# Moving GpSimd's elementwise work of a two-layer attention trunk to VectorE and ScalarE

## The chip, the cores and the metric

The kernel runs on one NeuronCore of a Trainium2 chip. The metric is device time in microseconds of one execution. The engines are named as in the profile: PE (TensorE matmul) and PEld (its weight loads), DVE (VectorE), ACT (ScalarE), POOL (GpSimd) and SP (SyncE, which here only issues DMAs). Every engine works through its own instructions in the order in which they were issued.

## The reference

Two layers over a sequence of 2048 rows of 1024 columns, in float32. Each layer normalises and modulates its rows, projects them, runs four heads of a gated linear recurrence (GLA) and four heads of differential softmax attention over all earlier rows, gates both with a SiLU, and projects the result back onto the rows.

```
for l in range(DEPTH):
    shift, scale, gate = split(silu(c) @ w_ada[l] + b_ada[l], 3)
    h = rms_norm(x, norm_g[l]) * (1 + scale) + shift
    gq, gk, gv, glr, gz, dq, dk, dv, dz = split_columns(h @ w_in[l])
    o_gla  = rms_norm(recurrence(gq, gk, gv, glr), gla_norm_g) * silu(gz)
    o_diff = rms_norm((softmax(q1 k1) - lam * softmax(q2 k2)) v) * (1 - lam_init) * silu(dz)
             # q and k of every head are rms-normed over 64 columns first
    x = x + gate * (concatenate([o_gla, o_diff]) @ w_out[l])
```

## The kernel before

**Units.** A unit is 512 rows (`u` = 0 to 3, four tiles `t` of 128 rows) of one layer `l`. For each unit the rows are normalised and transposed (`h`), projected in seven pieces of 512 columns (items 0 to 3: one attention head each; 4 and 5: the GLA's q, k and v; 6: its gate), put through the recurrence and the attention, and projected out in two halves of 512 columns (`out_gen`, items 7 and 8). Keys and values of earlier units come back from DRAM, so attention grows from unit 0 to unit 3.

**Split weights.** Dense products are made in three passes, `w` and `h` each being split into a rounded high part and the low part that is left: high by high, high by low, low by high. In unit 0 of a layer `weights` (L586) loads a piece `raw`, ACT rounds it into `hi`, POOL subtracts (`lo`, L596), and the pair is stored to DRAM (`wd`); units 1 to 3 load the finished pair. So `raw`, the 72 rounding casts of a layer and its 72 low parts stand in unit 0 alone.

**Roots.** GpSimd makes every reciprocal root with `pow(., -0.5)`: per tile of rows in `load_x` (xrs), per tile and head in `head_evac` (L910, `rq`, four columns), twice per unit in the recurrence (L868, `gw`, eight columns), and per query tile in the attention's `pv` (L1035, `wq`). In `head_evac` each tile's root is followed on DVE by the product that scales q and k (`rw`), and PE then transposes the four `rw`. In `gla_gen` the root `gw` is needed before the scaled output can leave PSUM into `osb` (the profile shows this buffer as `vN`).

**Gates.** `gate_proj` multiplies `osb` by the SiLU of the gate on POOL (L1107). `out_gen` multiplies each PSUM bank by the layer's `gate` on DVE into `t` and adds the residual `rt` on POOL (L1146 to L1152); in the last half of the last unit the add is on DVE. `gate` is itself made in four pieces by `ada_part(l, 2)`, which runs beside the projections.

**Order.** The code first only records instructions. Six generators (attention, q/k transposes, GLA, preparation, modulation, dense projections) are advanced against a rough clock (`run_streams`); `need` makes a generator wait until an event was recorded. `Program.order` then plays a list schedule with fixed costs and latencies per engine and issues everything in the order that comes out, so the order on every engine is fixed before the kernel runs, and a change of one instruction's engine re-plans the others. All DMAs are on SP's queue. `p_w` has four buffers of weight pairs, `p_raw` three, PSUM four accumulation banks (`acc`) and four for everything else (`sc`, `tp`, `po`).

In the profile nearly every instruction carries the line of the issuing helper (L305), so its tiles tell what it is: `w<-raw,w` is a low part, `rq<-qss,mhalf` a root, `rt<-t,rt` a residual add, `s<-s,r` the difference of the two softmax maps.

Of the kernel before, what the change touches and what calls it, by code (L numbers as in the profile page):

```python
# [11 lines left out]
F32 = mybir.dt.float32  # L12
F32R = mybir.dt.float32r
BF16 = mybir.dt.bfloat16
# [6 lines left out]
P = 128  # L21
# [287 lines left out]
def trunk_kernel(ctx, tc, x, c, w_ada, b_ada, norm_g, w_in, conv_w, w_gk, b_gk, gla_norm_g,  # L309
# [276 lines left out]
    def weights(l, u, item, k, src, n=None):  # L586
        w = p_w.tile([P, 2, 512], F32R, tag="w", name="w")
        hi, lo = w[:, 0, :], w[:, 1, :]
        kept = WD[l][item][k]
        if u > 0:  # L590
            SY.dma_start(w.bitcast(F32), kept)
            return hi, lo
        raw = p_raw.tile([P, 512], F32, tag="raw", name="raw")
        SY.dma_start(raw if n is None else raw.rearrange("p (g n) -> p g n", n=n), src)
        A.copy(hi, raw)
        G.tensor_tensor(lo, raw, hi.bitcast(F32), op=ALU.subtract)  # L596
        if NU > 1:
            SY.dma_start(kept, w.bitcast(F32))
        return hi, lo

    def silu2(dst, ps, shape=(P, 512)):
        th = t2(shape)
        A.activation(th, ps, AF.Tanh, scale=0.5)
        V.scalar_tensor_tensor(dst, th, 1.0, ps, op0=ALU.add, op1=ALU.mult)

# [124 lines left out]
    def gla_gen(l, u):  # L730
# [92 lines left out]
        for pr in range(TT // 2):  # L823
# [38 lines left out]
            for half in range(2):  # L862
# [13 lines left out]
        GL["osb"] = osb  # L876
        done("scan", key)
# [14 lines left out]
    def head_evac(l, u, hd, banks):  # L892
# [6 lines left out]
        for t in range(TT):  # L899
# [9 lines left out]
            V.tensor_scalar(ss[:, t, :], ss[:, t, :], 1.0 / 64, EPS, op0=ALU.mult, op1=ALU.add)  # L909
            G.tensor_tensor(rq[:, t, :], ss[:, t, :], mhalf[:, 0:4], op=ALU.pow)  # L910
            rv = rw.rearrange("p (a n) -> p a n", a=4)
            V.tensor_tensor(rv, rv, rq[:, t, :].unsqueeze(2).to_broadcast([P, 4, 64]), op=ALU.mult)
            qk.append(rw)
# [154 lines left out]
    def dense_gen(l, u, items):  # L1068
# [28 lines left out]
        def gate_proj():  # L1097
            banks = []
            yield from proj_N(lambda k: weights(l, u, 6, k, w_in[l, k * P:(k + 1) * P, C_GZ:C_GZ + 512]), banks)
            if LAST == 4:  # L1100
                done("free_h", key + 1)
            yield need("scan", key)
            osb = GL["osb"]
# [15 lines left out]
    def out_gen(l, u):  # L1119
# [3 lines left out]
        final = key == L * NU - 1  # L1123
        for hf in range(2):
# [119 lines left out]
```

## Time and profile before

| | |
|---|---|
| median of 3 runs | 2620.98 us (2617.81 to 2625.61) |
| the profiled execution, its own time | 2622.21 us |
| its span, first to last instruction | 2620.5 us |
| granted TensorE clock, mean | 0.992 |
| ACT busy | 1215.3 us (46%), 2592 instructions |
| HBM read, written | 362.29 MB, 111.15 MB |

The profile is of one execution; times of single instructions come from it. A group's row gives the number of instructions, the time in which at least one of them ran, the mean duration of one in ns, and, behind the second bar, how long the engine stood idle just before them and who ended that. Matmuls are pipelined, so their rows overlap. A row of stages gives, for each engine, busy time and number of instructions in a stretch of the span.

### The profile page before, as it was taken

What the parts mean: (1) busy time and instruction counts of PE and PEld (TensorE: products, weight loads), DVE (VectorE), ACT (ScalarE), POOL (GpSimd) and SP (SyncE); (2) the same over time, 40 slices, a digit from 0 to 9 for tenths busy, and PEclk for the clock granted to TensorE, in tenths of its full rate; (3) what the DMA queues carried; (4) which work ended last, traced back from release to release, by engine and by line L of the source; (5) the groups of instructions that cost most, each with busy time, mean ns of one, the idle gap of its engine ahead of it and who ended that gap; (6) DMA issues with size and microseconds to landing.
All of it is one profiled execution on the core that took longest, in us unless ns stands there. A gap on an engine that the chain in (4) does not pass through costs nothing.

```text
span 2620.5 us, 40701 instructions
## 1 busy us (share of the span) xinstructions
PE 2495.5 (95%) x13923; PEld 2031.5 (78%) x13923; DVE 1771.3 (68%) x5021; ACT 1215.3 (46%) x2592; POOL 608.3 (23%) x804
## 2 busy tenths in 40 slices
PE   6899899999999999999899999999999999999997
PEld 4676678877888778888677777888788887888786
DVE  4778847874667846677847874657737787377854
ACT  3555623554345543545634564344624556244442
POOL 2445421122010210102144554111111112110111
PEclk9999999999999999999999999999999999999998
DMA  8677586446553455344267767454374443743342
GB/s 283 225 235 256 200 302 198 161 166 211 178 181 125 158 171 189 133 140 149 81 237 248 245 214 253 169 179 156 126 268 155 143 157 113 254 141 129 101 149 89
DMA packets 201615, 476.11 MB, mean 182 GB/s; under 512 B 20736, under 2 KB 78272, under 8 KB 201408
## 3 DMA queue, kind: packets, MB, share of 16 engines
q1 hardware_dynamic: 201408, 473.51, 53.6%
q8 instruction: 111, 1.82, 0.3%
q14 instruction: 96, 0.79, 0.1%
HBM read 362.29 MB, written 111.15 MB: 181 GB/s over the span
## 4 chain that ended last, share of the span: by engine, by line
PE 71%; DVE 17%; DMA 3%; ACT 3%; issue 3%; POOL 1%; SPq 1%; DVEq 0%; ACTq 0%; POOLq 0%
PE acc L305 46%; PE sc L305 10%; PE po L305 8%; PE tp L305 7%; DVE s L305 6%; DVE t L305 3%; DMA wr<-in_w_ada_dram 1%; ACT s L305 1%; SPq L305 1%; DVE ql L305 1%; DVE am L305 1%; DVE hhi L305 1%; DMA w<-wd 1%; DVE r L305 1%; DVE hlo L305 1%
## 5 line engine op out<-in xcount | busy, mean ns | idle before, releaser
L305 PE MATMUL acc<-w,hhi 128*128 128x512 f32 x2560 | 835.0, 402 | 8.7 <-DMA w<-wd 4.3
L305 PEld LDWEIGHTS acc<-w,hhi 128*128 128x128 f32 x2560 | 464.8, 189 | 101.1 <-ACT ub L305 6.8
L305 PE MATMUL acc<-w,hlo 128*128 128x512 f32 x1280 | 504.9, 395 | 0.0
L305 ACT ACTIVATE s<-s,mx 128x512 f32<-128x512 f32 (+15 forms) x256 | 308.1, 1204 | 375.1 <-DVE s L305 372.3
L305 PE MATMUL acc<-hhi,w 128*128 128x512 f32 x1024 | 370.3, 402 | 0.6 <-DVE z L305 0.3
L305 PE MATMUL acc<-w,oh 128*128 128x512 f32 x1024 | 331.9, 401 | 12.1 <-DVE t L305 6.0
L305 DVE TENSOR_SCALAR_CACHE_REDUCE s<-sc,mx 64x64 f32<-64x64 f32 (+5 forms) x640 | 307.1, 485 | 37.8 <-PE sc L305 19.3
L305 POOL MEMSET s<- 64x64 f32 x256 | 38.9, 156 | 1111.1 <-DVE s L305 575.6
L305 PEld LDWEIGHTS acc<-w,hlo 128*128 128x128 f32 x1280 | 241.5, 189 | 48.9
L305 POOL TENSOR_TENSOR w<-raw,w 128x512 fp32r<-128x512 f32 x144 | 195.0, 1363 | 197.1 <-ACT w L305 180.7
L305 PEld LDWEIGHTS acc<-w,oh 128*128 128x128 f32 x1024 | 190.6, 190 | 55.8 <-DVE t L305 11.0
L305 PEld LDWEIGHTS acc<-hhi,w 128*128 128x128 f32 x1024 | 192.4, 188 | 37.7 <-DVE z L305 1.4
L305 PE MATMUL po<-Vj,aT 128*128 128x128 f32 x1536 | 207.9, 280 | 13.1 <-ACT aT L305 12.2
L305 PEld LDWEIGHTS po<-Vj,aT 128*128 128x128 f32 x1536 | 193.7, 195 | 24.6 <-ACT aT L305 18.9
L305 ACT COPY aT<-tp 128x512 f32<-128x512 f32 (+2 forms) x320 | 162.4, 520 | 94.1 <-PE tp L305 90.6
L305 PE MATMUL acc<-w,ol 128*128 128x512 f32 x512 | 202.8, 401 | 1.2 <-DVE ol L305 1.1
L305 DVE TENSOR_SCALAR_CACHE_REDUCE s<-sc 128x512 f32<-128x512 f32 (+4 forms) x256 | 158.6, 623 | 65.7 <-PE sc L305 61.6
L305 DVE SCALAR_TENSOR_TENSOR s<-s,r 128x512 f32<-128x512 f32 (+2 forms) x320 | 200.7, 677 | 3.1
L305 PE MATMUL acc<-hlo,w 128*128 128x512 f32 x512 | 200.9, 392 | 0.0
L305 PE MATMUL tp<-ident,s 128*128 128x128 f32 x1088 | 171.8, 275 | 16.9 <-DVE s L305 11.6
L305 POOL TENSOR_TENSOR rq<-qss,mhalf 128x4 f32<-128x4 f32 x128 | 129.8, 1032 | 215.4 <-DVE qss L305 215.3
L305 PEld LDWEIGHTS tp<-ident,s 128*128 128x128 f32 x1088 | 130.5, 140 | 55.4 <-issue 12.3
(177 smaller groups left out, 4064.7 us busy)
## 6 DMA issues: line engine op xcount, KB each, us to landing
w<-wd SPq DMA_DIRECT2D x432, 512.0 KB
wd<-w SPq DMA_DIRECT2D x144, 512.0 KB
raw<-in_w_in_dram SPq DMA_DIRECT2D x112, 256.0 KB
Kj<-kd SPq DMA_DIRECT2D x48, 512.0 KB
wr<-in_w_ada_dram SPq DMA_DIRECT2D x128, 128.0 KB
kd<-Kt SPq DMA_DIRECT2D x24, 512.0 KB
Vj<-vd SPq DMA_DIRECT2D x48, 256.0 KB
xt<-in_x_dram SPq DMA_DIRECT2D x16, 512.0 KB
```

Of the source, the lines that this page charges most:

```text
L305: getattr(self.engines[e], method)(*[real(a) for a in args], **{k: real(v) for k, v in kw.items()})
```

## The change

- **Low parts** of the weights (`lo`) are subtracted on DVE instead of POOL.
- **The residual gate goes into `w_out`.** For items 7 and 8 of unit 0, DVE multiplies `raw` by the matching 512 columns of `gate` before the cast; the stored pairs then hold the gated weights. `out_gen` has no product with `gate` any more: one DVE add takes the PSUM bank and the residual. The wait for `ada_part(l, 2)` moves from the end of each half to the start of `out_gen`.
- **Roots of q and k** are made once per head over 16 columns by the new `rsqrt` on DVE: a starting value by integer arithmetic on the float's bits, then three Newton steps, twelve instructions in all. The four `rw` products follow it.
- **The GLA's output** is copied unscaled from PSUM into `osb` by ACT. Its root is made once per unit by `rsqrt`, over 16 columns, and the scale is joined with the gate: per tile and head one DVE instruction multiplies `osb` by the root and by the SiLU.
- `pow` stays on POOL for `xrs` and `wq`, and so do the fills of `s`.

```
@@ weights
+        if item >= 7:
+            V.tensor_tensor(raw, raw, layers[l].gate[:, (item - 7) * 512:(item - 6) * 512], op=ALU.mult)
         A.copy(hi, raw)
-        G.tensor_tensor(lo, raw, hi.bitcast(F32), op=ALU.subtract)
+        V.tensor_tensor(lo, raw, hi.bitcast(F32), op=ALU.subtract)
@@
+    def rsqrt(y, x, scale, eps):
+        n = x.shape[1]
+        V.tensor_scalar(x, x, -0.5 * scale, -0.5 * eps, op0=ALU.mult, op1=ALU.add)
+        b = p_sm.tile([P, n], F32, tag=f"nb{n}", name="nb", bufs=2)
+        V.tensor_scalar(b, x, -2.0, None, op0=ALU.mult)
+        V.tensor_scalar(y.bitcast(I32), b.bitcast(I32), -0.5, float(0x5f3759df), op0=ALU.mult, op1=ALU.add)
+        for _ in range(3):
+            V.tensor_tensor(b, y, y, op=ALU.mult)
+            V.tensor_tensor(b, b, x, op=ALU.mult)
+            V.scalar_tensor_tensor(y, b, 1.5, y, op0=ALU.add, op1=ALU.mult)
@@ gla_gen
-            V.tensor_scalar(ss[:, ts_, :], ss[:, ts_, :], 1.0 / P, 4096.0 * EPS, op0=ALU.mult, op1=ALU.add)
-            G.tensor_tensor(wv[:, ts_, :].rearrange("p t a -> p (t a)"), ss[:, ts_, :].rearrange("p t a -> p (t a)"),
-                            mhalf[:, 0:8], op=ALU.pow)
             for half in range(2):
-                V.tensor_tensor(osb[:, ts_, :].rearrange("p t (a b n) -> p b t a n", b=2, n=P)[:, half],
-                                ops_[half].rearrange("p (t a n) -> p t a n", t=2, a=2),
-                                wv[:, ts_, 2 * half:2 * half + 2].unsqueeze(3).to_broadcast([P, 2, 2, P]), op=ALU.mult)
+                A.copy(osb[:, ts_, :].rearrange("p t (a b n) -> p b t a n", b=2, n=P)[:, half],
+                       ops_[half].rearrange("p (t a n) -> p t a n", t=2, a=2))
...
+        rsqrt(wv.rearrange("p t a -> p (t a)"), ss.rearrange("p t a -> p (t a)"), 1.0 / P, 4096.0 * EPS)
@@ head_evac, per tile t
-            V.tensor_scalar(ss[:, t, :], ss[:, t, :], 1.0 / 64, EPS, op0=ALU.mult, op1=ALU.add)
-            G.tensor_tensor(rq[:, t, :], ss[:, t, :], mhalf[:, 0:4], op=ALU.pow)
...
+        rsqrt(rq.rearrange("p t a -> p (t a)"), ss.rearrange("p t a -> p (t a)"), 1.0 / 64, EPS)
+        for t in range(TT):
+            rv = qk[t].rearrange("p (a n) -> p a n", a=4)
             V.tensor_tensor(rv, rv, rq[:, t, :].unsqueeze(2).to_broadcast([P, 4, 64]), op=ALU.mult)
@@ gate_proj
-                G.tensor_tensor(osb[:, t, :], osb[:, t, :], sz, op=ALU.mult)
+                for hd in range(4):
+                    hs = slice(hd * P, hd * P + P)
+                    V.scalar_tensor_tensor(osb[:, t, hs], osb[:, t, hs], wv[:, t, 2 * (hd % 2) + hd // 2:][:, 0:1],
+                                           sz[:, hs], op0=ALU.mult, op1=ALU.mult)
@@ out_gen
+        yield need("ada", l, 2)
         for hf in range(2):
...
-            yield need("ada", l, 2)
...
-                gy = t2()
-                V.tensor_tensor(gy, banks[t], y.gate[:, cs], op=ALU.mult)
+                V.tensor_tensor(rt[:, t, :], banks[t], rt[:, t, :], op=ALU.add)
                 if final and hf == 1:
-                    V.tensor_tensor(rt[:, t, :], gy, rt[:, t, :], op=ALU.add)
                     SY.dma_start(xo[:, t, :], rt[:, t, :])
-                    continue
-                G.tensor_tensor(rt[:, t, :], gy, rt[:, t, :], op=ALU.add)
-                if t % 2:
+                elif t % 2:
                     SY.dma_start(xo[:, t - 1:t + 1, :], rt[:, t - 1:t + 1, :])
```

Three places of the issued order show what moves. First POOL, from the roots of the first unit's rows on, before:

```order
L305 TENSOR_TENSOR xrs<-xss,mhalf 128x1 x4
L305 TENSOR_TENSOR w<-raw,w 128x512 x3
L305 MEMSET s 64x64 x4
L305 TENSOR_TENSOR w<-raw,w 128x512 x6
L305 TENSOR_TENSOR rq<-qss,mhalf 128x4 x4
L305 TENSOR_TENSOR w<-raw,w 128x512 x6
```

and with the change:

```order
L306 TENSOR_TENSOR xrs<-xss,mhalf 128x1 x4
L306 MEMSET s 64x64 x7
L306 TENSOR_TENSOR wq<-oss,mhalf 128x1
L306 MEMSET s 64x64
L306 TENSOR_TENSOR wq<-oss,mhalf 128x1
```

Low parts and roots of q and k are gone from POOL; fills of `s` and the roots `wq` of the attention's output follow one another.

Second DVE, in unit 0 of the first layer, where a head's q and k are normalised while the recurrence's states (`Sn`) are made, before (`am` belongs to the making of `gate`):

```order
L305 TENSOR_REDUCE qss<-sq 128x4
L305 SCALAR_TENSOR_TENSOR am<-wr,cact,am 128x256
L305 TENSOR_SCALAR qss<-qss 128x4
L305 SCALAR_TENSOR_TENSOR am<-wr,cact,am 128x256
L305 SCALAR_TENSOR_TENSOR Sn<-Sn,a_sb,sc 128x128 x5
L305 TENSOR_TENSOR vN<-po,gw 128x4x128
L305 SCALAR_TENSOR_TENSOR Sn<-Sn,a_sb,sc 128x128
L305 TENSOR_TENSOR vN<-po,gw 128x4x128
L305 TENSOR_TENSOR rw<-rw,rq 128x256 x2
```

and with the change the same place begins so:

```order
L306 TENSOR_REDUCE qss<-sq 128x4
L306 SCALAR_TENSOR_TENSOR am<-wr,cact,am 128x256
L306 TENSOR_SCALAR qss<-qss 128x16
L306 TENSOR_TENSOR w<-raw,w 128x512
L306 TENSOR_SCALAR nb<-qss 128x16
L306 TENSOR_TENSOR w<-raw,w 128x512
L306 TENSOR_SCALAR rq<-nb 128x16
L306 SCALAR_TENSOR_TENSOR Sn<-Sn,a_sb,sc 128x128
L306 TENSOR_TENSOR nb<-rq 128x16
L306 SCALAR_TENSOR_TENSOR Sn<-Sn,a_sb,sc 128x128
L306 TENSOR_TENSOR nb<-nb,qss 128x16
L306 SCALAR_TENSOR_TENSOR Sn<-Sn,a_sb,sc 128x128
```

The twelve root instructions alternate with state updates and low parts, and all four `rw` come behind them. Third DVE at the end of the program, the last half's evacuation, before:

```order
L305 TENSOR_TENSOR ol<-oT,oh 128x512 x7
L305 TENSOR_TENSOR t_26728<-acc,gate_14008 128x512
L305 TENSOR_TENSOR t_26733<-acc,gate_14008 128x512
L305 TENSOR_TENSOR rt<-t_26728,rt 128x512
L305 TENSOR_TENSOR rt<-t_26733,rt 128x512
L305 TENSOR_TENSOR t_26743<-acc,gate_14008 128x512
L305 TENSOR_TENSOR t_26746<-acc,gate_14008 128x512
L305 TENSOR_TENSOR rt<-t_26743,rt 128x512
L305 TENSOR_TENSOR rt<-t_26746,rt 128x512
```

and with the change:

```order
L306 SCALAR_TENSOR_TENSOR oss<-oss,r 128x1
L306 SCALAR_TENSOR_TENSOR z<-po,wq,z 128x128
L306 TENSOR_TENSOR ol<-oT,oh 128x512 x2
L306 TENSOR_TENSOR rt<-acc,rt 128x512 x4
L306 TENSOR_TENSOR ol<-oT,oh 128x512 x7
L306 TENSOR_TENSOR rt<-acc,rt 128x512 x4
```

Eight instructions behind the last product become four. On PE the order hardly moves: the first product of `out_gen` of unit 0 is the 825th row of the issued order before and the 828th with the change.

More of the change, by code (lines that the diff above doesn't have):

```diff
@@ L13 @@
 F32R = mybir.dt.float32r
+I32 = mybir.dt.int32
 BF16 = mybir.dt.bfloat16
@@ L876, in gla_gen @@
         GL["osb"] = osb
+        rsqrt(wv.rearrange("p t a -> p (t a)"), ss.rearrange("p t a -> p (t a)"), 1.0 / P, 4096.0 * EPS)
+        GL["wv"] = wv
         done("scan", key)
@@ L908, in head_evac @@
             V.tensor_reduce(ss[:, t, :], sq.rearrange("p (a n) -> p a n", a=4), axis=AX.X, op=ALU.add)
-            V.tensor_scalar(ss[:, t, :], ss[:, t, :], 1.0 / 64, EPS, op0=ALU.mult, op1=ALU.add)
-            G.tensor_tensor(rq[:, t, :], ss[:, t, :], mhalf[:, 0:4], op=ALU.pow)
-            rv = rw.rearrange("p (a n) -> p a n", a=4)
+            qk.append(rw)
+        rsqrt(rq.rearrange("p t a -> p (t a)"), ss.rearrange("p t a -> p (t a)"), 1.0 / 64, EPS)
+        for t in range(TT):
+            rv = qk[t].rearrange("p (a n) -> p a n", a=4)
             V.tensor_tensor(rv, rv, rq[:, t, :].unsqueeze(2).to_broadcast([P, 4, 64]), op=ALU.mult)
-            qk.append(rw)
         HD[key, hd] = (qk, Vt, sz)
@@ L1102, in gate_proj @@
             yield need("scan", key)
-            osb = GL["osb"]
+            osb, wv = GL["osb"], GL["wv"]
             for t in range(TT):
```

## The prediction

> **What bounds the kernel now.** I read the page's busy shares first, then the chain of work that ended last, then the table of stages.
>
> ```profile
> span 2620.5 us, 40701 instructions
> ## 1 busy us (share of the span) xinstructions
> PE 2495.5 (95%) x13923; PEld 2031.5 (78%) x13923; DVE 1771.3 (68%) x5021; ACT 1215.3 (46%) x2592; POOL 608.3 (23%) x804
> ```
>
> ```profile
> PE 71%; DVE 17%; DMA 3%; ACT 3%; issue 3%; POOL 1%; SPq 1%; DVEq 0%; ACTq 0%; POOLq 0%
> ```
>
> PE is busy 95% of the span, and POOL, the engine that is relieved, is 1% of the chain. So emptying POOL pays little by itself. What counts is whether PE waits less. The stages, unit 0 of both layers (first two rows) against unit 2 of both (last two), say where it waits:
>
> ```profile
> 66.00:330.00 264.00, 237.32 (x1239) 182.58 (x1240) 206.78 (x527) 149.38 (x352) 130.48 (x140) 0.99 0.69 231
> 1320.00:1584.00 264.00, 247.76 (x1284) 195.80 (x1284) 187.98 (x497) 133.64 (x332) 136.17 (x145) 0.99 0.71 241
> 660.00:924.00 264.00, 261.33 (x1545) 218.46 (x1544) 198.06 (x593) 131.37 (x277) 40.31 (x70) 1.00 0.47 158
> 1914.00:2178.00 264.00, 261.53 (x1503) 217.91 (x1502) 182.73 (x541) 114.12 (x245) 43.16 (x68) 1.00 0.49 166
> ```
>
> The columns are the length and the busy time of PE, PEld, DVE, ACT and POOL. In unit 2 PE idles 2.6 us of 264. In unit 0 it idles 26.7 and 16.2, together 42.9, or 37.7 more than two stretches of unit 2. POOL is busy three times as long there. Later units can hardly gain, unit 0 can.
>
> [...]
>
> How POOL gets in PE's way stands in one place of the timeline, in unit 0 of layer 0:
>
> ```profile
> 204.68 2.70 POOL L305 TENSOR_TENSOR w<-raw,w 128x512 fp32r<-128x512 f32 x2
> ...
> 205.21 2.45 DVE L305 TENSOR_TENSOR rw<-rw,rq 128x256 f32<-128x256 f32 x2
> ...
> 206.30 0.33 PE L305 MATMUL tp<-ident,rw 128*128 128x128 f32 x1 [0.68 <-DVE rw L305]
> ...
> 207.71 0.33 PE L305 MATMUL tp<-ident,rw 128*128 128x128 f32 x1 [0.85 <-DVE rw L305]
> ```
>
> Two `rw` products take 2.45 us while POOL makes two low parts, and PE idles 0.68 and 0.85 us for them. In the same two stages of layer 0 the 16 `rw` (with nothing else of DVE on that tile) read
>
> ```profile
> 66.00:330.00 264.00, 5.54 (x32) 3.87 (x32) 12.57 (x16) 12.62 (x32) 0.99 0.69 231
> ...
> 660.00:924.00 264.00, 4.79 (x32) 3.96 (x32) 6.71 (x16) 12.11 (x32) 1.00 0.47 158
> ```
>
> DVE is the third time here: 0.79 us each in unit 0, 0.42 in unit 2, so the pair above lost 1.6 us, and PE idled 1.53 for it. A POOL product over 512 columns holds up a DVE instruction that reads two SBUF tensors.
>
> **The size of this stretching.** Means of the groups beside their own medians (the middle of three durations, ns):
>
> ```profile
> L305 DVE TENSOR_TENSOR ol<-oT,oh 128x512 fp32r<-128x512 f32 x128 | 98.1, 770 | 103.7 <-ACT oh L305 103.5
> L305 DVE SCALAR_TENSOR_TENSOR am<-wr,cact,am 128x256 f32<-128x256 f32 x112 | 66.9, 597 | 35.5 <-DMA wr<-in_w_ada_dram 34.2
> ...
> L305 DVE TENSOR_TENSOR t<-acc,gate 128x512 f32<-128x512 f32 x64 | 42.5, 687 | 24.4 <-PE acc L305 23.2 <-PE sc L305 1.1
> ...
> L305 DVE SCALAR_TENSOR_TENSOR oss<-oss,r 128x1 f32<-128x1 f32 x128 | 33.6, 263 | 63.6 <-ACT junk L305 63.2
> ...
> L305 DVE TENSOR_TENSOR vN<-po,gw 128x512 f32<-128x512 f32 x32 | 21.7, 686 | 7.9 <-POOL gw L305 7.8
> ...
> L305 DVE TENSOR_SCALAR qss<-qss 128x4 f32<-128x4 f32 x128 | 20.9, 165 | 0.5
> ...
> L305 DVE SCALAR_TENSOR_TENSOR s<-s,r 128x128 f32<-128x128 f32 x32 | 11.1, 347 | 0.1
> ```
>
> ```profile
> L305 DVE TENSOR_TENSOR ol<-oT,oh x128: 676/691/1779, 123.7 to 2609.4; 128x512 fp32r<-128x512 f32 x128
> ```
>
> ```profile
> L305 DVE SCALAR_TENSOR_TENSOR am<-wr,cact,am x112: 464/484/1583, 27.7 to 1445.2; 128x256 f32<-128x256 f32 x112
> ```
>
> ```profile
> L305 DVE SCALAR_TENSOR_TENSOR oss<-oss,r x128: 141/156/1261, 97.8 to 2584.5; 128x1 f32<-128x1 f32 x128
> ```
>
> The excess is 128 x 79 ns = 10.1 us for `ol`, 112 x 113 = 12.7 for `am`, 128 x 107 = 13.7 for `oss`, and 32 x 0.37 = 12 for the `rw` of two units 0 by the stage row: 48 us in four groups. How much of it PE feels lies between nothing and the smaller of 48 and the 37.7 us of idle time that unit 0 has too much. The pair above passed nearly all; but much else (`ol`, `am`) is made well ahead. I take a little over half: **22 us gained**.
>
> **What POOL loses.**
>
> ```profile
> L305 POOL TENSOR_TENSOR w<-raw,w 128x512 fp32r<-128x512 f32 x144 | 195.0, 1363 | 197.1 <-ACT w L305 180.7 <-DMA kd<-Kt 5.6 <-DMA raw<-in_w_in_dram 3.6
> L305 POOL TENSOR_TENSOR rq<-qss,mhalf 128x4 f32<-128x4 f32 x128 | 129.8, 1032 | 215.4 <-DVE qss L305 215.3
> L305 POOL TENSOR_TENSOR rt<-t,rt 128x512 f32<-128x512 f32 x60 | 81.4, 1388 | 164.7 <-DVE t L305 96.0 <-DMA w<-wd 47.5 <-issue 20.6
> ...
> L305 POOL TENSOR_TENSOR vN<-vN,t 128x512 f32<-128x512 f32 x32 | 41.6, 1317 | 15.7 <-DVE t L305 14.1 <-DVE oss L305 1.5
> ```
>
> 195.0 + 129.8 + 81.4 + 41.6 = 448 of 608 us go. PE itself waited for POOL's work seldom:
>
> ```profile
> PE acc L305 <- POOL w L305: 3.0, 3, 1.9
> ```
>
> **3 us gained**, if the low parts come no later from DVE.
>
> **What DVE gets.** A DVE instruction holds its engine for less than it lasts:
>
> ```profile
> 200.89 0.16 DVE L305 TENSOR_SCALAR gss<-gss 128x8 f32<-128x8 f32 x1
> 200.96 0.16 DVE L305 TENSOR_SCALAR qss<-qss 128x4 f32<-128x4 f32 x1
> 201.03 0.28 DVE L305 SCALAR_TENSOR_TENSOR z<-th,acc 128x128 f32<-128x128 f32 x1
> ```
>
> ```profile
> 2614.88 1.28 DVE L305 TENSOR_TENSOR t<-acc,gate 128x512 f32<-128x512 f32 x2
> 2616.08 1.28 DVE L305 TENSOR_TENSOR rt<-t,rt 128x512 f32<-128x512 f32 x2
> ```
>
> Small ones start 0.07 us apart; two of 512 columns take 1.28, so one holds the engine 0.60. Added: 144 low parts and 32 products on `w_out`, 176 x 0.60 = 106 us; 60 residual adds, 36; 128 scale-and-gate products at 0.347 less the 0.09 by which the small rows overlap (0.16 - 0.07), 33; 40 roots (32 heads, 8 units) of 12 steps, 480 x 0.07 = 34 us if others stand between the steps (as the order shows) and 480 x 0.165 = 79 if each waits for the one before. No row has a step of 16 columns; I take 50, nearer the spacing row, and keep both ends. Removed: 64 products with `gate`, 38; 32 `vN`, 19; 128 `qss` preparations, 9. Sum 106 + 36 + 33 + 50 - 66 = 159 us more, less the stretching of 48: about 110, so 1880 us, 72%.
>
> In units 1 to 3 this is some 10 us a unit, and DVE idles 66 us and more of each 264 there: I cost it at nothing; the cover is the rest of PE's work, and were it gone the price would be those 10 us. ACT's 32 additional copies lie in its idle half. In unit 0 a layer gets 72 x 0.60 + 16 x 0.60 + 5 roots of 1.25 + 4 = 63 us on a DVE busy 207 of 264, and loses the stretching. There PE idled 42.9 us for 394.8 us of DVE work, 0.11 per us; at that rate two times 63 cost **14 us**. From below the price is nothing, if the products of PE that stand ready cover it; from above it is the slower rival's.
>
> The root's place costs nothing in my sum: before, each tile's `rw` waited for its own root of 1.03 us; now four `rw` follow twelve steps of 0.16 each, about 2 us. PE's transposes of `rw` come under dense products. The longer preparation of `w_out` (product, cast, low part in a row) is prefetched like the loads it follows.
>
> **The tail.** The last PE row starts at 2613.94; before, four more DVE instructions stand behind it up to 2617.36 (2616.08 + 1.28). With the change one add of 0.69 follows the last bank, so about 2615.2: **2 us gained**.
>
> Sum: -22 - 3 - 2 + 14 = -13 us on the profiled execution's own 2622.2, so **2609 us**. That execution stands 1.2 us above the median of three.
>
> **Rivals.** (a) *The stretching was most of unit 0's loss.* Then the idle excess of 37.7 goes, with the 5 of POOL and tail, and DVE's new work is covered: 2579. For it: the `rw` pair. Against: most gaps of unit 0 are ended by chains of ACT and DVE that attention over few keys would have anyway.
> (b) *One trade for another.* DVE's new work costs PE in unit 0 what the stretching did (22 against 22); tail and POOL's 5 remain: 2617, no change. For it: 88 new instructions of 0.60 us per unit 0, each able to stand in front of a short `oss` or `r`, just like POOL's before.
> (c) *Slower: DVE stands where POOL stood.* POOL waited 180.7 us for ACT's casts ahead of its low parts, and only low parts were behind it. Now all of DVE's work is behind such a wait, and behind the casts are the landings of `raw`. If a quarter of that wait appears on DVE (45 us) and passes to PE, with the 14 above and the gains of 27 against it: 2654; at a tenth, 2627. It decides for slower from some 20 us of DVE idle time ended by ACT's `w`. Against: the issued order places a low part when its cast is due, with other work ahead.
> (d) *The contention stays.* 160 us of roots and fills remain on POOL. [...] The trace shows the stretching under 512-column products alone, so this is inside the range.
>
> **Chances.** My forecast's case (gain of 8 to 27 us) 0.36, (a) 0.12, (b) and its neighbourhood 0.30, (c) 0.22. A difference under 0.3% (8 us) can't be told from none here. Faster 0.48, same 0.30, slower 0.22. The range leaves out half of (a) and the far half of (c): 2583 to 2640.
>
> **What would show it.** Right: means of `oss` and `am` fall to their medians, PE's idle time in unit 0 falls from 42.9 us to some 30, DVE's busy time is near 1880. Wrong: idle time before `w<-raw,w` on DVE in the tens of us (c), PE's idle in unit 0 unchanged (b), or PE waiting for `rw` or `w` in the list of waits, which would mean that the roots or the preparation of `w_out` come late.

## The result, and the profile after

| | before | after |
|---|---|---|
| median | 2619.39 us (2617.61 to 2625.61) | 2593.07 us (2590.53 to 2595.51) |
| ratio to before | 1 | 0.9895 (0.9874 to 0.9916) |
| the profiled execution's own time, span | 2622.2, 2620.5 us | 2595.51, 2593.6 us |

The change gains 26.3 us, or 1.05%. The forecast was 13 us; direction and range held, the size was half. The page after, its busy line and its chain of work that ended last:

```profile
span 2593.6 us, 40832 instructions
## 1 busy us (share of the span) xinstructions
PE 2491.5 (96%) x13923; PEld 2037.1 (79%) x13923; DVE 1841.1 (71%) x5625; ACT 1230.1 (47%) x2624; POOL 145.1 (6%) x424
...
PE 74%; DVE 15%; DMA 4%; ACT 3%; issue 2%; SPq 1%; POOL 0%; DVEq 0%; POOLq 0%; ACTq 0%
```

PE does the same 13923 products; span less busy time is its idle time, and that fell from 2620.5 - 2495.5 = 125.0 us to 102.1. DVE has 604 instructions more and only 69.8 us more busy time. The stages of before, in the same four windows (length, then PE, PEld, DVE, ACT, POOL; the clock is the number ahead of the DMA share):

```profile
66.00:330.00 264.00, 244.29 (x1276) 188.68 (x1274) 224.77 (x670) 152.85 (x359) 18.99 (x52) 0.99 0.72 247
1320.00:1584.00 264.00, 249.85 (x1299) 199.66 (x1298) 207.60 (x624) 144.63 (x348) 19.15 (x52) 0.97 0.70 239
660.00:924.00 264.00, 260.94 (x1569) 219.91 (x1569) 205.55 (x659) 135.05 (x277) 17.52 (x51) 1.00 0.46 153
1914.00:2178.00 264.00, 262.06 (x1542) 219.86 (x1541) 201.03 (x644) 131.50 (x278) 15.84 (x47) 1.00 0.46 160
```

In unit 0 PE now idles 19.7 and 14.2 us, together 33.9 where it was 42.9. That is 9 of the 23 us of idle time that went; the rest lies outside these windows. (The windows are cut at the same times, so in layer 1 they hold work that before came some 15 us later.) DVE's groups that were stretched, and the new one that waits for ACT (count, busy us, mean ns, idle time before and its releaser):

```profile
L306 DVE TENSOR_TENSOR w<-raw,w 128x512 fp32r<-128x512 f32 x144 | 98.5, 687 | 30.9 <-ACT w L306 30.2
L306 DVE TENSOR_TENSOR ol<-oT,oh 128x512 fp32r<-128x512 f32 x128 | 87.5, 688 | 88.0 <-ACT oh L306 85.7 <-PE acc L306 2.1
...
L306 DVE SCALAR_TENSOR_TENSOR am<-wr,cact,am 128x256 f32<-128x256 f32 x112 | 53.9, 482 | 24.8 <-DMA wr<-in_w_ada_dram 24.0
...
L306 DVE TENSOR_TENSOR rw<-rw,rq 128x256 f32<-128x256 f32 x128 | 45.8, 420 | 0.9
...
L306 DVE SCALAR_TENSOR_TENSOR oss<-oss,r 128x1 f32<-128x1 f32 x128 | 19.9, 155 | 55.6 <-ACT junk L306 55.1
```

`ol` fell from 770 to 688 ns, `am` from 597 to 482, `rw` from 498 to 420, `oss` from 263 to 155: the groups stand at the medians that they had before. Taken over every DVE instruction (its duration less the median of its group, in the packed trace), those that ran beside a POOL product of 512 columns lasted some 95 us too long in all before, and nothing after; beside a pow or a fill of `s` and no such product none lasted more than 0.04 us over its group's median in either.

Where the time was gained, read off one event that every unit has: the start of the last product with `ol` (the end of its output projection), in us from the span's start.

| layer, unit | 0, 0 | 0, 1 | 0, 2 | 0, 3 | 1, 0 | 1, 1 | 1, 2 | 1, 3 |
|---|---|---|---|---|---|---|---|---|
| before | 339.5 | 644.0 | 973.4 | 1348.1 | 1623.4 | 1919.9 | 2245.0 | 2613.9 |
| after | 329.4 | 635.5 | 960.0 | 1332.6 | 1605.5 | 1899.7 | 2222.8 | 2589.5 |
| after less before | -10.1 | -8.5 | -13.4 | -15.5 | -17.9 | -20.2 | -22.2 | -24.4 |

The steps between neighbouring columns are the gain of a unit. The two units 0 bring 10.1 + 2.4 = 12.5 us, the six later units 11.9 together, and what follows the last product 2.4. So close to half of the gain arose where the prediction had said that hardly any could. The table compares one execution of each kernel, and executions of one kernel differ by some us, so a single step is not exact.

One such place, the output projection of unit 2 of layer 0. The first two fences are before: a row of the timeline of PE, then windows (columns as in the stages above); the third is after, over the same work.

```profile
952.83 0.73 PE L305 MATMUL acc<-w,oh 128*128 128x512 f32 x2 [2.00 <-DVE t L305]
```

```profile
950.80:954.20 3.40, 1.40 (x7) 1.14 (x7) 2.48 (x6) 0.00 (x0) 1.34 (x2) 1.00 0.41 156
954.20:957.60 3.40, 3.40 (x10) 2.71 (x9) 1.27 (x2) 1.23 (x2) 1.22 (x1) 0.52 0.60 200
```

```profile
931.50:961.50 30.00, 30.00 (x138) 24.06 (x137) 16.16 (x30) 12.18 (x18) 0.00 (x0) 1.00 0.78 259
```

Before, PE waited 2.00 us for `t`, the product of a bank with `gate`, then ran the next 3.4 us at a granted clock of 0.52. After, the same projection runs 30 us without a gap and at full clock. The offset in the table moves by 4.9 us here. DVE was not idle ahead of that `t`: it had just made an `ol` of 1.34 us beside POOL's residual adds (its median is 0.69) and seven small instructions for the next layer's weights (`wgk`, `wb`, `wglr`). After, the four adds stand ahead of those small ones. How much of the 2.00 us is stretching and how much is the order isn't separated.

The tail, in the timeline of DVE after:

```profile
2587.87 2.73 DVE L306 TENSOR_TENSOR rt<-acc,rt 128x512 f32<-128x512 f32 x4 [2.28 <-PE acc L306]
```

One add per bank is left behind the last product.

### The profile page after: what moved, and what is told of

Same layout as the page of the kernel before. It is cut to its first block, busy times and chain, and to the rows that moved or that the text cites. A ratio compares the mean times of both kernels' runs of the same rounds, so it can differ in the third digit from the quotient of the medians.

```text
span 2593.6 us, 40832 instructions
## 1 busy us (share of the span) xinstructions
PE 2491.5 (96%) x13923; PEld 2037.1 (79%) x13923; DVE 1841.1 (71%) x5625; ACT 1230.1 (47%) x2624; POOL 145.1 (6%) x424
## 4 chain that ended last, share of the span: by engine, by line
PE 74%; DVE 15%; DMA 4%; ACT 3%; issue 2%; SPq 1%; POOL 0%; DVEq 0%; POOLq 0%; ACTq 0%
PE acc L306 48%; PE sc L306 10%; PE po L306 9%; PE tp L306 7%; DVE s L306 5%; DVE t L306 2%; DVE ql L306 1%; DMA wr<-in_w_ada_dram 1%; ACT s L306 1%; DVE w L306 1%; SPq L306 1%; DVE vN L306 1%; ACT qh L306 1%; DVE Kt L306 1%; DMA xt<-in_x_dram 1%
## 5 line engine op out<-in xcount | busy, mean ns | idle before, releaser
L306 PE MATMUL acc<-w,oh 128*128 128x512 f32 x1024 | 329.3, 401 | 11.6 <-ACT w L306 4.2
L306 PE MATMUL po<-Vj,aT 128*128 128x128 f32 x1536 | 209.2, 281 | 11.9 <-ACT aT L306 11.3
L306 PE MATMUL acc<-w,ol 128*128 128x512 f32 x512 | 197.1, 398 | 0.0
L306 PE MATMUL tp<-ident,s 128*128 128x128 f32 x1088 | 174.8, 276 | 21.8 <-DVE s L306 15.5
L306 PEld LDWEIGHTS tp<-ident,s 128*128 128x128 f32 x1088 | 131.3, 141 | 61.8 <-issue 20.7
L306 PE MATMUL sc<-Kj,qh 128*128 128x512 f32 x384 | 157.7, 411 | 2.1 <-ACT oT L306 0.7
L306 PE MATMUL sc<-Kj,ql 128*128 128x512 f32 x384 | 150.7, 392 | 0.0
L306 DVE TENSOR_TENSOR ol<-oT,oh 128x512 fp32r<-128x512 f32 x128 | 87.5, 688 | 88.0 <-ACT oh L306 85.7
```

The source lines that it names most:

```text
L306: getattr(self.engines[e], method)(*[real(a) for a in args], **{k: real(v) for k, v in kw.items()})
```

## The experiments

All start from the changed kernel. "Against after" is the difference of the medians; ratios are to the kernel before, on the same chip, where its median was 2618.57 to 2620.53 us. extra_pool and extra_fill add POOL work that nothing uses, newton6 three more Newton steps to each root. The clock is used in the last section.

| kernel | median us | ratio (interval) | against after | granted clock |
|---|---|---|---|---|
| low_pool | 2626.48 | 1.0023 (1.0011 to 1.0035) | +33.4 | 0.988 |
| extra_pool | 2663.09 | 1.0153 (1.0131 to 1.0174) | +70.0 | 0.985 |
| extra_fill | 2608.28 | 0.9959 (0.9945 to 0.9973) | +15.2 | 0.989 |
| gla_back | 2606.55 | 0.9946 (0.9931 to 0.9961) | +13.5 | 0.992 |
| gla_gate_dve | 2594.26 | 0.9898 (0.9883 to 0.9913) | +1.2 | 0.990 |
| out_back | 2590.26 | 0.9883 (0.9869 to 0.9898) | -2.8 | 0.993 |
| out_resid_dve | 2589.93 | 0.9897 (0.9882 to 0.9911) | -3.1 | 0.994 |
| roots_back | 2579.44 | 0.9847 (0.9832 to 0.9862) | -13.6 | 0.995 |
| roots_late | 2582.90 | 0.9863 (0.9847 to 0.9879) | -10.2 | 0.993 |
| newton6 | 2603.99 | 0.9945 (0.9932 to 0.9958) | +10.9 | 0.992 |
| roots_out_back | 2586.96 | 0.9879 (0.9861 to 0.9897) | -6.1 | 0.992 |
| roots_qact | 2594.22 | 0.9906 (0.9892 to 0.9920) | +1.2 | 0.989 |

Where each kernel gained or lost, by the start of the last `ol` product of every unit, against the changed kernel (one execution each):

| layer, unit | 0, 0 | 0, 1 | 0, 2 | 0, 3 | 1, 0 | 1, 1 | 1, 2 | 1, 3 |
|---|---|---|---|---|---|---|---|---|
| low_pool | 22.8 | 18.4 | 17.4 | 18.2 | 31.5 | 30.5 | 31.3 | 31.7 |
| extra_pool | 36.8 | 36.3 | 35.7 | 35.7 | 66.6 | 67.7 | 67.3 | 67.7 |
| gla_back | -0.8 | -1.2 | 0.5 | 5.4 | 6.3 | 7.4 | 11.6 | 11.0 |
| out_back | -6.9 | -7.4 | -2.5 | -0.7 | -5.2 | -6.8 | -5.0 | -7.3 |
| roots_back | -7.6 | -5.2 | -6.7 | -7.1 | -11.3 | -13.0 | -13.8 | -17.9 |
| roots_late | -7.1 | -10.1 | -11.6 | -12.3 | -12.2 | -13.3 | -13.5 | -13.1 |
| newton6 | 7.1 | 7.6 | 8.1 | 11.0 | 8.4 | 6.6 | 8.4 | 6.2 |

### Low parts back on POOL

```diff
-        V.tensor_tensor(lo, raw, hi.bitcast(F32), op=ALU.subtract)
+        G.tensor_tensor(lo, raw, hi.bitcast(F32), op=ALU.subtract)
```

> The changed kernel with the 144 low parts back on POOL, all else as changed. Contention theory (a POOL product over 512 columns holds up DVE instructions that read two SBUF tensors, and PE waits for those): the low parts are 144 of the 236 products that left POOL, so some 60% of the gain goes back, 2606 us, and the means of oss and am rise again from about 156 and 484 ns to well over 200 and 550. Evacuation theory (the gain comes from fewer and shorter steps behind the projections, not from contention): 2593 us within 4, since the low parts are not behind any projection. Load theory (new DVE work costs PE time in unit 0): faster than the changed kernel, 2585 or less.

2626.48 us: all of the gain is gone and more. In the groups of DVE and in the list of PE's waits (us in total, times, longest):

```profile
L306 DVE SCALAR_TENSOR_TENSOR am<-wr,cact,am 128x256 f32<-128x256 f32 x112 | 68.5, 611 | 28.7 <-DMA wr<-in_w_ada_dram 27.6
...
L306 DVE SCALAR_TENSOR_TENSOR oss<-oss,r 128x1 f32<-128x1 f32 x128 | 27.6, 215 | 56.6 <-ACT junk L306 56.2
```

```profile
PE tp L306 <- DVE rw L306: 14.2, 9, 2.5
```

The stretching is back (`am` 611 ns against 482), and PE waits 14.2 us for `rw`, 1.4 in the changed kernel. The sign is that of the contention theory, the size far above it; the loss lies in the two units 0, where the low parts are. Of the 14.2 us a part belongs to the pair of edits: the kernel before had the stretching too, but no chain of steps ahead of `rw`, and waited 2.3.

### The same POOL products, with nothing taken from DVE

In extra_pool DVE keeps its low parts and POOL makes the same product beside them, into a buffer that nobody reads again; in extra_fill POOL is kept busy with two fills instead, which read no SBUF tensor.

```diff
         V.tensor_tensor(lo, raw, hi.bitcast(F32), op=ALU.subtract)
+        G.tensor_tensor(raw, raw, hi.bitcast(F32), op=ALU.subtract)   # extra_pool
+        G.memset(raw, 0.0)                                            # extra_fill, twice
```

> The changed kernel, low parts on DVE, and beside each of them one more POOL product over 512 columns that nobody needs (raw minus its rounded part, written back into raw). POOL thus works as much as with the low parts on it, but no result that is used comes from it; a raw buffer comes free some 1.4 us later. Contention theory: the stretching returns, most of the 33 us that the low parts on POOL cost comes back, 2615 us or more. Queue theory (what cost the time is that roots and fills for the attention stood behind low parts in POOL's queue): the same, so this run alone can't tell the two apart, its twin does. Latency theory (the low part itself came 0.8 us later from POOL): 2593 us within 4.

> As the run with the additional POOL product, but with two fills of raw (128 x 512) instead, which read nothing from SBUF. POOL is occupied for about as long per low part, and raw is held as long; the profile before shows no stretching of DVE beside fills. Contention theory: oss and am keep their medians of 156 and 484 ns, 2593 to 2598 us. Queue theory: as slow as its twin.

Groups and PE's waits of extra_pool, then of extra_fill:

```profile
L306 POOL TENSOR_TENSOR raw<-raw,w 128x512 f32<-128x512 f32 x144 | 211.0, 1469 | 359.0 <-DVE w L306 211.6 <-issue 41.0 <-DVE nb L306 27.4
```

```profile
L306 DVE SCALAR_TENSOR_TENSOR am<-wr,cact,am 128x256 f32<-128x256 f32 x112 | 65.7, 586 | 25.5 <-DMA wr<-in_w_ada_dram 24.5
```

```profile
PE tp L306 <- DVE s L306: 25.5, 27, 2.7
PE tp L306 <- DVE rw L306: 13.8, 7, 3.6
```

```profile
L306 POOL MEMSET raw<- 128x512 f32 x288 | 149.1, 530 | 351.3 <-DVE w L306 287.9 <-ACT w L306 17.3 <-ACT t L306 16.7
```

```profile
L306 DVE SCALAR_TENSOR_TENSOR oss<-oss,r 128x1 f32<-128x1 f32 x128 | 19.8, 155 | 56.8 <-ACT junk L306 56.3
```

```profile
PE tp L306 <- DVE s L306: 11.3, 18, 1.6
...
PE tp L306 <- DVE rw L306: 1.6, 3, 0.7
```

With the products `am` lasts 586 ns again, and all of the loss lies in the two units 0. The fills leave DVE's groups of two SBUF inputs at their means of the changed kernel (`oss` 155 ns, `am` 481, `ol` 688, `rw` 420). A few instructions of one input they stretch, by 6 us in all, as the duration's least, median and most show for one of the root's steps (median 174 in the changed kernel, most 177):

```profile
L306 DVE TENSOR_SCALAR rq<-nb x32: 164/175/617, 78.4 to 2465.5; 128x16 int32<-128x16 int32 x32
```

PE's waits for `s` fall and those for `rw` stay. Still the fills cost 15 us, where 0 to 5 were expected. PE's waits for casts and low parts (ACT's and DVE's `w`) rise from 4.7 + 4.2 to 10.0 + 7.5 us; this fits the buffer `raw` coming free later, which no run tests by itself. The queue theory is out as the main cause: with fills in the queue PE waits for `z`, which hangs on POOL's `wq`, no longer than in the changed kernel (4.4 us against 4.5, at transposes). The products cost 2663.09 - 2608.28 = 54.8 us more than the fills, for 81 us by which they stretch DVE's instructions. The two differ in length too (211 us against 149), so this isn't a pure price of contention, but PE's waits for `s` and `rw`, 12.9 in sum with fills and 39.3 with products, are where about half of the difference passes. 144 products are then 0.38 us each.

### The gate of the linear attention

gla_back makes root, scale and gate as before, the gate product on POOL; gla_gate_dve differs from it in the engine of that one product.

```diff
-                    V.scalar_tensor_tensor(osb[:, t, hs], osb[:, t, hs], wv[...], sz[:, hs], ...)
+                G.tensor_tensor(osb[:, t, :], osb[:, t, :], sz, op=ALU.mult)   # gla_back
+                V.tensor_tensor(osb[:, t, :], osb[:, t, :], sz, op=ALU.mult)   # gla_gate_dve
```

> The changed kernel with the GLA's scaling as before: root by pow on POOL over eight columns, scale on DVE out of PSUM, gate product on POOL (32 products of 512 columns). Contention theory: 32 of 236 products return, 3 us, 2596 us. Evacuation theory (the PSUM banks of the recurrence were held 5 us for the root, and the gate product was four POOL products in a row ahead of the transposes): 2599 us or more. Otherwise 2593 us within 4.

> The changed kernel with the GLA's root by pow on POOL and its scale on DVE out of PSUM as before, but the gate product on DVE (512 columns) and not on POOL. The GLA's part as a whole was worth 13 us (2606.5 against 2593). Contention theory: the 32 POOL products are what cost, so 2593 to 2597 us. Round-trip theory (the root's way over POOL, with the recurrence's PSUM banks held meanwhile): stays at 2603 us or more.

13.5 us against 1.2, as the contention theory of the second expectation had it: the joined scale, the copies on ACT and the late root are worth nothing (gla_back alone, in the range of the evacuation theory, could not tell), and 32 products on POOL 12.3 us, 0.38 us each again, for 19 us of stretching. Nearly all of it comes in units 1 to 3 (6.2 and 4.7 us in the table). One place of gla_back in unit 2 of layer 1, in the timelines of POOL, DVE and PE:

```profile
2161.06 1.41 POOL L306 TENSOR_TENSOR vN<-vN,t 128x512 f32<-128x512 f32 x1 [1.16 <-DVE t L306]
...
2163.84 1.28 POOL L306 TENSOR_TENSOR vN<-vN,t 128x512 f32<-128x512 f32 x1 [0.72 <-DVE t L306]
```

```profile
2161.24 1.25 DVE L306 SCALAR_TENSOR_TENSOR oss<-oss,r 128x1 f32<-128x1 f32 x1
...
2163.68 1.58 DVE L306 CAST hhi<-t 128x256 fp32r<-128x256 f32 x2
2165.19 0.34 DVE L306 SCALAR_TENSOR_TENSOR z<-po,wq,z 128x128 f32<-128x128 f32 x1
```

```profile
2165.58 0.50 PE L306 MATMUL sc<-Kj,qh 128*128 128x512 f32 x1 [1.04 <-DVE z L306]
```

A one-column `oss` starts 0.18 us after the POOL product and ends with it, 1.1 us late, and all that follows on DVE moves with it. A pair of casts beside the next POOL product takes 1.58 us (0.29 each in the changed kernel). `z` stands behind both, and PE idles 1.04 us for it; the root `wq` between them had ended at 2163.12 and wasn't what held it. Whether all 12 us are of this kind, or some come from the gate's four products in a row on a slower engine (1.35 us each on POOL, 0.68 on DVE in gla_gate_dve), isn't separated.

### The output projection

out_back takes the gate out of `w_out` and gives it back to the banks, with the residual add on POOL; out_resid_dve is the same with the add on DVE.

```diff
-        if item >= 7:
-            V.tensor_tensor(raw, raw, layers[l].gate[:, ...], op=ALU.mult)
...
-                V.tensor_tensor(rt[:, t, :], banks[t], rt[:, t, :], op=ALU.add)
+                gy = t2()
+                V.tensor_tensor(gy, banks[t], y.gate[:, cs], op=ALU.mult)
+                G.tensor_tensor(rt[:, t, :], gy, rt[:, t, :], op=ALU.add)   # out_back
+                V.tensor_tensor(rt[:, t, :], gy, rt[:, t, :], op=ALU.add)   # out_resid_dve
```

> The changed kernel with the output projection as before: w_out not gated, product with gate on DVE, residual add on POOL (60 products of 512 columns). Contention theory: 60 of 236 products return, a quarter of the gain, about 2600 us, and the mean of ol rises from 688 to about 770 ns, in all units. Evacuation theory: half of the gain or more, 2606 to 2613 us, at the borders between the halves of the output projection in units 1 to 3. Load theory: the product with gate and the add together cost DVE no more than the product on w_out and the add, so nothing.

> The changed kernel with w_out not gated: product with gate and residual add are both on DVE, no POOL work in the output projection. Against the run with the old output projection (2590 us) only the 60 adds move from POOL to DVE. Contention theory: POOL's 60 products cost there at the GLA's rate of 0.4 us each; taking them away is worth up to 24 us less the price of 36 us more DVE work (12 us at 0.32), so 2578 to 2586 us. If POOL's products stand where DVE has little to do (the output projection), they cost nothing and the adds cost DVE little too: 2590 us within 4.

Both come out level with the changed kernel. For out_back this is the load theory's "nothing"; the contention and evacuation theories missed, though the stretching did return (`ol` 722 ns, 12.5 us over all of DVE). For out_resid_dve it is the second theory: 60 products of 512 columns on POOL or on DVE made no difference here. The row of out_back in the table shows why a part that does much can be worth nothing. Without the product on `w_out` unit 0 of layer 0 is 6.9 us shorter. In its output projection the changed kernel's PE waits 5.5 us for casts and low parts (ACT's and DVE's `w`, 255 to 345 us), the longest

```profile
292.98 0.91 PE L306 MATMUL acc<-w,oh 128*128 128x512 f32 x2 [2.69 <-ACT w L306]
```

and out_back's PE not at all. Of the 6.9 us, 4.9 are lost again in unit 2. There PE waits for `t` just as before the change (timelines of PE, DVE and POOL of out_back):

```profile
938.29 0.73 PE L306 MATMUL acc<-w,oh 128*128 128x512 f32 x2 [2.02 <-DVE t L306]
```

```profile
933.10 0.69 DVE L306 TENSOR_TENSOR t<-acc,gate 128x512 f32<-128x512 f32 x1 [0.67 <-POOL rt L306]
933.71 2.08 DVE L306 CAST wgk<-t 32x256 fp32r<-32x256 f32 x2
...
937.56 0.68 DVE L306 TENSOR_TENSOR t<-acc,gate 128x512 f32<-128x512 f32 x1
```

```profile
931.77 3.87 POOL L306 TENSOR_TENSOR rt<-t,rt 128x512 f32<-128x512 f32 x3 [13.87 <-DVE t L306]
```

POOL's adds get in the way twice: the third `t` waits 0.67 us for one, and a pair of small casts beside them takes 2.08 us, where it takes 0.59 in the changed kernel. The fourth `t`, for which PE waits, stands behind those casts in DVE's order. With the adds on DVE PE's waits for `t` in this projection are 1.4 us in two pieces; the medians of the two kernels agree.

### The roots of the heads

roots_back gives each tile's root back to POOL's pow. roots_late does too, but with one DVE copy behind the four, so that the products on `rw` begin together as in the changed kernel; it tells the load of the steps from their place. newton6 doubles the steps of every root (heads and linear attention, 360 more).

```diff
-        rsqrt(rq..., ss..., 1.0 / 64, EPS)
+            V.tensor_scalar(ss[:, t, :], ss[:, t, :], 1.0 / 64, EPS, op0=ALU.mult, op1=ALU.add)
+            G.tensor_tensor(rq[:, t, :], ss[:, t, :], mhalf[:, 0:4], op=ALU.pow)   # roots_back, roots_late
+        V.tensor_copy(ss..., rq...)                                                # roots_late, once a head
...
-        for _ in range(3):
+        for _ in range(6):                                                         # newton6
```

> The changed kernel with the roots of q and k back on POOL as pow, one per tile (128 of them), all else as changed. Contention theory: pow over four columns stretches nothing, so 2593 us within 4. Round-trip theory (DVE stands still for POOL's roots, 18.8 us before, and what is behind waits): 2600 us or more. Load theory (384 small DVE steps cost PE time): 2588 us or less.

> Low parts, GLA and output projection as changed, roots of q and k by pow on POOL, one per tile, but the four rw products wait for all four roots, by one small DVE copy of 16 columns per head (32 copies in all). Without that wait the same kernel took 2579 us. Load theory: 2579 to 2582 us. Batching theory: back to 2590 us or more.

> The changed kernel with six Newton steps in place of three: 360 more DVE instructions on 16 columns. The roots on DVE cost 13.6 us against pow on POOL, with some 43 us more DVE busy time, 0.32 us of PE's time per us of DVE. Load theory: 360 more of them at 0.1 to 0.165 us cost 36 to 60 us of DVE and 12 to 19 us of time, 2605 to 2612 us. Batching theory (what costs is that the four rw products wait for the last tile's sum and come in one row): the chain gets longer by 9 steps per head only, under dense products, so 2593 to 2597 us.

13.6 us faster without the Newton steps, 10.2 with the pow and the late start, 10.9 slower with twice the steps. The load theory comes within 1.1 us of all three, the batching theory misses the last two. So it is their time on DVE, not where they stand. The group of steps in newton6, then PE's wait for `s` in newton6 and in roots_back:

```profile
L306 DVE SCALAR_TENSOR_TENSOR rq<-nb,rq 128x16 f32<-128x16 f32 x192 | 33.4, 174 | 4.5
```

```profile
PE tp L306 <- DVE s L306: 20.7, 26, 3.2
```

```profile
PE tp L306 <- DVE s L306: 10.9, 19, 1.5
```

Between them stands the changed kernel with 15.5 (and roots_late with 9.4). PE hardly waits for the roots (for `rw` 1.4 us in the changed kernel); it waits more for `s`, the softmax products that stand among the steps on DVE. That is a part of the cost only, 4.6 of 18 us between the two spans, and out_back, with all the steps on DVE, has 11.7: where the rest passes isn't shown. newton6's DVE has 1891.5 - 1841.1 = 50.4 us more to do and the kernel 10.9 more to run, 0.22 us for each; from roots_back to the changed kernel it is 42.6 and 13.6, 0.32 for each.

In roots_back DVE waits 13.7 us for POOL's `rq` at the head of `rw`, and POOL's pow stretches nothing:

```profile
L306 DVE TENSOR_TENSOR rw<-rw,rq 128x256 f32<-128x256 f32 x128 | 53.8, 421 | 14.4 <-POOL rq L306 13.7
```

The changed kernel, which has no such pow, has 420 ns. Of these 128 products 85 ran beside a pow (medians 419 ns beside one, 424 alone); in the kernel before 80 beside a pow and no product had a median of 418 ns and the 10 beside a product of 512 columns one of 1495. DVE's wait passes nothing on: PE's list of waits has no row for `rw` in roots_back. **roots_back is the fastest version, 1.5% below before and 0.5% below the changed kernel.**

### Two attempts to go further

roots_out_back joins roots_back and out_back. roots_qact is roots_back with the 128 copies between the halves of `qh` and `ql` on ACT:

```diff
-                    V.tensor_copy(qh[other, m, :], qh[own, m, :].bitcast(F32))
-                    V.tensor_copy(ql[other, m, :], ql[own, m, :].bitcast(F32))
+                    A.copy(qh[other, m, :], qh[own, m, :].bitcast(F32))
+                    A.copy(ql[other, m, :], ql[own, m, :].bitcast(F32))
```

> The changed kernel with both the roots of q and k on POOL (pow) and the output projection as before; low parts and the GLA's part as changed. If the parts add up as measured one by one (-13.6 and -2.8 against the changed kernel): 2577 us. If the output projection's 60 POOL products stretch more when roots stand on POOL too: 2585 us or more.

> The fastest version so far (roots of q and k on POOL, 2579 us) with the 128 copies of q's halves (64 x 512, 0.42 us each, 54 us of DVE) moved from DVE to ACT. Load theory at 0.32 us per us of DVE: 17 us less, 2562 us. Rival (ACT is on the chain for q and for the softmax, and a copy lasts longer there, 0.58 us): 2579 us or more.

Neither gained. roots_out_back, 2586.96, is 7.5 us slower than roots_back: the parts don't add up. The rival had named the time, but not the reason: POOL's products stretch DVE by 13.6 us there and by 12.5 in out_back (what does show is in the last section). roots_qact took 48 us of work from DVE (1798.5 to 1750.5) and lost 15 us, as its rival had it. In PE's waits, roots_qact and then roots_back:

```profile
PE sc L306 <- DVE Kt L306: 11.2, 16, 1.5
```

```profile
PE sc L306 <- DVE Kt L306: 4.6, 10, 0.6
```

The copies now stand on ACT ahead of the chain that makes `Kt`: DVE idles 50.2 us for ACT's `Kt`, 1.9 for anything ahead of it in roots_back, and PE waits there. That is 6.6 of the 15 us; the rest isn't traced, but half of the loss shows as granted clock (last section). DVE's total is no price list: 0.22 to 0.32 us per us held for the steps, not for these copies.

## Why the prediction was half right

**"A little over half" of 48 us: 22 us gained.** The mechanism is right, the term mis-sized. Four parts undone one at a time cost +33.4 (low parts), +13.5 (linear attention), -13.6 (roots of the heads) and -2.8 us (output): 30.5 in sum, against 26.3 measured, so they nearly add up from here. The 33.4 is net of DVE's relief: 144 low parts at the 0.60 us of the prediction are 86 us, and at 0.22 to 0.32 us per us 19 to 28, so the stretching by low parts would be some 52 to 61, around the 54.8 between extra_pool and extra_fill. That is an estimate, and part of it is the pairing with the Newton steps told of above. The stretching by the gate products adds 12. Two steps failed here. The excess was summed over four groups only; others had it as well. Before, then after:

```profile
L305 DVE SCALAR_TENSOR_TENSOR t<-ub,vec,t 128x512 f32<-128x512 f32 x192 | 148.0, 771 | 1.0
...
L305 DVE TENSOR_TENSOR hlo<-t,hhi 128x256 fp32r<-128x256 f32 x128 | 55.4, 456 | 1.1
...
L305 DVE CAST hhi<-t 128x256 fp32r<-128x256 f32 x128 | 45.0, 375 | 7.0 <-ACT t L305 6.8
```

```profile
L306 DVE SCALAR_TENSOR_TENSOR t<-ub,vec,t 128x512 f32<-128x512 f32 x192 | 143.5, 747 | 1.0
...
L306 DVE TENSOR_TENSOR hlo<-t,hhi 128x256 fp32r<-128x256 f32 x128 | 50.4, 420 | 0.5
...
L306 DVE CAST hhi<-t 128x256 fp32r<-128x256 f32 x128 | 33.5, 289 | 5.6 <-ACT t L306 5.5
```

These three alone add 148.0 - 143.5 + 55.4 - 50.4 + 45.0 - 33.5 = 21 us, and all groups together 95, twice the 48 of the sum. The cast among them has one SBUF input, so "a DVE instruction that reads two SBUF tensors" was too narrow as well. And the bound, "the smaller of 48 and the 37.7 us of idle time that unit 0 has too much", took PE's loss to be idle time in unit 0 beyond that of unit 2. Later units had stalls too, and extra_pool loses 67.7 us in units 0 alone. A stall can also cost clock behind it (0.52 in the window above), but the change gained none by that: (1 - clock) x span is 18.5 us on average over the 37 executions of the kernel before in the experiments, and 20.7 over the four of the changed kernel.

**"Later units can hardly gain, unit 0 can."** Wrong: 11.9 of 26.8 us came in units 1 to 3. POOL's gate products cost there (gla_back loses 10.9 of its 11.0 us in units 1 to 3), and so do the banks that wait for `t`. A window of 264 us inside a unit's attention shows neither: the windows ended ahead of the output projection.

**"14 us" for DVE's new work, at 0.11 us per us.** Half or less of what was measured where it can be read, 0.22 in newton6 and 0.32 for the roots of the heads. The rate came from PE's idle time over all of DVE's work in unit 0, an average; added work was dearer.

**"The root's place costs nothing"** is borne out for the place: roots_late, with it, gives only 3.5 us less than roots_back, inside their intervals. The load, which the sum had inside 14 us and in unit 0 alone, was not covered: 13.6 us for the 32 roots of the heads. Whether "I cost it at nothing" held for units 1 to 3 stays open. The rows of roots_back, roots_late and newton6 agree on the first unit, 7.1 to 7.6 us, and not on the rest: in the later units of layer 0 the steps cost -0.5, 5.2 and 3.9 us, in those of layer 1 6.6, 0.9 and -2.2.

**"Prefetched like the loads it follows"** for `w_out` was wrong in layer 0: PE's 5.5 us of waits there, and the 6.9 us less of out_back in that unit. The saved evacuation pays it back, which the sum had not counted either. Two errors that cancelled, which is luck.

**The tail, 2 us**: 2.4. **DVE's busy time near 1880**: 1841.1, because 95 us of stretching went and not 48 (159 - 95 = 64 us more, 69.8 measured). **PE idle in unit 0 of some 30**: 33.9.

**Rivals.** (c) appeared and didn't decide. DVE idles 30.2 us ended by ACT's `w`, over the 20 from which it should have made the kernel slower; PE's waits for low parts and casts stayed small, 8.9 us where casts and low parts had cost 4.2 before (after, list of waits):

```profile
PE acc L306 <- ACT w L306: 4.7, 3, 2.7
...
PE acc L306 <- DVE w L306: 4.2, 3, 2.9
```

So "passes to PE" was the failing step: here 30.2 us of DVE's idle time went with at most 4.7 more of PE's. (a), 2579, took the stretching for all of unit 0's loss; roots_back reaches that number, but with 18 of its 42 us outside the units 0. (d), stretching by the roots and fills that stay, fell: `oss` and `am` are at their medians after. The fills of extra_fill left `oss` at 155 ns, and the pows of roots_back, 1.03 us each, left `rw` at 421; in gla_back one `oss` beside a product of 1.41 us lasted 1.25 us.

## What to carry to other kernels

Price an elementwise product on a helper engine by what it holds up on the engine that feeds the bottleneck, over every group that this engine runs and in every stage: here a 512-column POOL product among low parts or gates cost about 0.38 us of the kernel, 60 residual adds cost no more on POOL than on DVE, and small pows and 64-column fills stretched nothing by more than 0.04 us. When such work is moved, add the new load at the place where the bottleneck waits (here in part softmax products among Newton steps), and move only what contends: leaving the cheap pow where it was made the kernel faster than moving all of it. Undo the parts one by one before believing a total, since a part worth nothing may be two large terms that cancel.

## What was not expected of the hardware

In the traces of before and after the granted clock of PE is 1.00 or 0.50 at any time, each stretch at 0.50 that ends in the trace lasts 3.41 or 6.83 us, and a piece of that 3.4 us need not be idle to be followed by half clock. Windows of the changed kernel (columns as above):

```profile
1395.90:1399.30 3.40, 0.68 (x5) 0.42 (x4) 3.40 (x7) 0.61 (x1) 0.00 (x0) 1.00 0.27 77
1399.30:1402.70 3.40, 1.82 (x4) 1.49 (x5) 3.40 (x7) 0.63 (x1) 0.00 (x0) 0.50 0.42 150
1402.70:1406.10 3.40, 3.40 (x11) 2.73 (x10) 2.01 (x6) 0.62 (x1) 0.00 (x0) 0.50 1.02 319
```

A piece with PE 20% busy, then two at 0.50. Counted over the pieces of 3.41 us of these two traces, from the first record of the clock on, by the share of a piece in which a product's record runs: after full clock all 15 pieces under 40% were followed by half clock, none of 1434 above 70%, and 7 of 38 between; after half clock all 5 under 80% were followed by another half, and none of 19 above 90%.

In each of the two all half-clock pieces begin on one grid of 3.41 us, and it stands at another offset to the first instruction (2.0 us in the kernel before, 3.2 in the changed one). That the same stall costs more or less by where it falls on the grid is an estimate from this; no run tests it. Executions of one kernel would fit: of the kernel before one took 2612.24 us at a clock of 0.996 and another 2625.30 at 0.990, 13 us apart where (1 - clock) x span is 16 apart.

The lost clock, (1 - clock) x span, comes to 1.7 us for each half-clock piece. It is 0.005 x 2575.7 = 13 us in the profiled execution of roots_back, 23 in that of the changed kernel, 29 in roots_qact and 40 in extra_pool. So 10 of the 18 us between these two spans of roots_back and the changed kernel show as clock, but the two are the fastest and the slowest execution of their kernels. Averaged over all executions on record the lost clock is 16.1 us in roots_back, 20.7 in the changed kernel, 17.5 in out_back, 22.0 in roots_out_back and 23.3 in roots_qact: 5 of 13 us between the first two, 6 of the 8 by which roots_out_back is behind roots_back, and 7 of 14 for roots_qact. Outside of it the parts add up to within 2 us: roots_back, out_back and roots_out_back are 8.4, 0.3 and 6.6 us ahead of the changed kernel. How much of the clock follows from more stalls and how much from where they fall is open.
